# Split weights made by GpSimd for the expert blocks computed ahead, and 34 of them instead of 30

## The chip, the core and the metric

The kernel runs on one core of one Trainium2 chip. A core has a matrix engine (TensorE, PE in the rows, with its weight loads shown apart as PEld), three engines for elementwise work (VectorE or DVE, ScalarE or ACT, GpSimd or POOL), a queue engine that issues transfers (SyncE or SP) and 16 DMA engines. The metric is the device time of one execution in microseconds (us).

## The reference

One decoder layer on 512 tokens of width 1024 in float32. First a mixer (a gated linear recurrence beside sparse attention), then an expert layer, then a gated embedding. What the change touches is the expert layer:

```python
q = (xt @ wq).reshape(128, 8, 2, 128)                       # 8 heads, two half queries
s = einsum('thcd,hckd->thck', q, sub_keys)                  # key scores, 128 keys a half
top_s, top_i = top_k(s, 16)
best_s, best_c = top_k(all sums of the two halves, 16)      # 16 experts of 16384 for each token and head
expert = i1 * 128 + i2
w = softmax(best_s)
act = gelu(einsum('thkd,td->thk', u[expert], xt))
out = einsum('thk,thkd->td', w * act, v[expert])
```

## The kernel before

Tokens stand in four tiles of 128. For the last three tiles (TD = 384 tokens) nothing is gathered: the kernel multiplies all 16384 rows of u and v, in 128 blocks of 128 experts. For block b it loads uT[b] (128x1024, 512 KB, tile `ur`), forms u x for the 384 tokens in PSUM (`apsum`), takes the gelu of it on ScalarE (tile `gp` or `ga`), multiplies that by the routing weights of the block (`wt`) and multiplies the product by v[b] into six accumulators (`ac`). The first token tile is done by gathering: GpSimd issues 256 indirect loads of rows, and VectorE does a dot product or a scaled add with each.

A float32 product can be made in two ways here. With `full`, TensorE takes the float32 tiles as they are, one matmul instruction for each of the 8 chunks, which the trace shows as two records each. Otherwise a tile is split into a high part (a copy that rounds to fp32r) and a low part (what is left), and `mm3` makes three fast matmuls for each chunk: high by high, high by low, low by high. `split` (lines 186 and 187) makes the high part on ScalarE and the low part on VectorE. The tokens are split beforehand (`xTh`, `xTl`).

The stages around the change are these. After the key scores of the last head (a loop over `hc`, with the top 16 taken by VectorE on each), XB = 6 full blocks are issued behind the last score matmul. Meanwhile `route(1)` works on VectorE and ScalarE: it combines the two top-16 lists of token tile 1 and finds expert numbers. `dense_tile` for token tiles 1, 2 and 3 then turns the expert numbers into a dense weight array: VectorE makes one-hot arrays `o1`, `o2` and their products `oh`, `ol` (128x2048 f16, two buffers each), TensorE multiplies them (`wm`, lines 979 and 980), ScalarE evicts (`hn`, `stage`), a DMA writes them to DRAM (`wd`). Between two groups of 32 such matmuls a generator, `a_steps`, issues three chunks of an expert block, so that TensorE has work while it waits for one-hots; `route(2)` and `route(3)` are woven in too. For tiles 1 and 2 (FT = 3) these blocks are full, for tile 3 split. Blocks still missing up to NPRE = 30 come after, split; the last HOLD = 3 of them load and store through GpSimd's queue, all others through SP's. The gelu of the first AHEAD = 10 blocks stays in SBUF, that of blocks 10 to NPRE - 1 goes to DRAM (`gd`) and comes back. Last, a loop over all 128 blocks does the products with v and, from block NPRE on, also the split u products one block ahead; the gathering for token tile 0 is spread over blocks NPRE to 124.

`ur`, `uh` and `ul` have two buffers each, so a block's tiles wait until TensorE is done with the block two before it. Each engine runs its instructions in the order in which the scheduler wrote them. In the block below, line 783 is the full product and line 779 the split.

Of the kernel before, what the change touches and what calls it, by code (L numbers as in the profile page):

```python
# [10 lines left out]
F32 = mybir.dt.float32  # L11
# [5 lines left out]
AF = mybir.ActivationFunctionType  # L17
ALU = mybir.AluOpType
# [23 lines left out]
FT = 3  # L42
# [24 lines left out]
PLAN = [("b",0),("b",1),("c",),("a",3,(1,2,0),4),("p",),("a",3,(1,2,0),8),("a",3,(1,2,0),ALL),("l",0),("o",0,2),("o",0,0),("o",0,1),("a",2,(1,2,0),5),("a",2,(1,2,0),ALL),("o",0,3),("l",1),("a",1,(0,1,2),ALL),("o",1,3),("o",1,2),("a",0,(0,1,2),3),("a",0,(0,1,2),ALL),("o",1,1)]  # L67
POST = [("n",3),("o",0),("n",2),("n",1),("n",0)]
APRI = 150
XB = 6  # L70
NP = 3
NPRE = 30
STARTS = [sum(16 // (k + 1) for k in range(i)) for i in range(17)]
NCAND = STARTS[16]

# [79 lines left out]
def _body(ctx, tc, a, out, dbg=None):  # L155
    nc = tc.nc
    V, S, G, PE = nc.vector, nc.scalar, nc.gpsimd, nc.tensor
    act = S.activation
# [21 lines left out]
    def mm3(o, lh, ll, rh, rl, first, last):  # L180
        PE.matmul(o, lhsT=lh, rhs=rh, start=first, stop=False)  # L181
        PE.matmul(o, lhsT=lh, rhs=rl, start=False, stop=False)  # L182
        return PE.matmul(o, lhsT=ll, rhs=rh, start=False, stop=last)  # L183

    def split(hi, lo, src):
        act(hi, src, AF.Copy)  # L186
        return V.tensor_tensor(lo, src, hi.bitcast(F32), op=ALU.subtract)  # L187

    def flat(ap):
        return ap.rearrange("p a b -> p (a b)")  # L190
# [336 lines left out]
    with ExitStack() as e2:  # L527
# [170 lines left out]
        for step in PLAN:  # L698
            if step[0] == "a":
                tt, order, n = step[1:]  # L700
# [30 lines left out]
    SH = [128, QH, 16, 16]  # L731
    gd = dram.tile([max(NPRE - AHEAD, 1), 128, TD], F32, name="gd")
    wd = [dram.tile([n_, 128, TD // 32, 128], F32, name=f"wd{k}") for k, n_ in enumerate((WFIRST, NB // 4 - WFIRST))]
# [34 lines left out]
    def a_steps(full):  # L768
        b = nextb[0]
        nextb[0] += 1  # L770
        dq = nc.gpsimd if NPRE - HOLD <= b < NPRE else nc.sync
        ur = dense.tile([128, NC, 128], F32, name="ur")
        dq.dma_start(out=ur, in_=a["uT"][b])
        g_ = prep.tile([128, TD], F32, name="gp") if b < AHEAD else dense.tile([128, TD], F32, name="ga", bufs=3)
        ahead.append(g_ if b < AHEAD or b >= NPRE else None)
        if not full:
            uh = dense.tile([128, NC, 128], F32R, name="uh")
            ul = dense.tile([128, NC, 128], F32R, name="ul")
            split(flat(uh), flat(ul), flat(ur))
        o = aps.tile([128, 512], F32, name="apsum")  # L780
        for c in range(NC):
            if full:
                PE.matmul(o[:, :TD], lhsT=ur[:, c], rhs=xf[:, c], start=c == 0, stop=c == NC - 1)  # L783
            else:
                mm3(o[:, :TD], uh[:, c], ul[:, c], xTh[:, c, T - TD:], xTl[:, c, T - TD:], c == 0, c == NC - 1)
            if c < NC - 1:
                yield
        act(g_, o[:, :TD], AF.Gelu_apprx_tanh)  # L788
        if AHEAD <= b < NPRE:
            dq.dma_start(out=gd[b - AHEAD], in_=g_)  # L790

    def a_block(full=False):
        if nextb[0] < NB:
            for _ in a_steps(full):
                pass
# [71 lines left out]
    with ExitStack() as e2:  # L867
# [4 lines left out]
        with ExitStack() as e3:  # L872
# [40 lines left out]
                        V.max_index(ti[tt][:, h, 8:16], tv[tt][:, h, 8:16], rep)  # L913
            with tc.issue_after(last.ins):
                for _ in range(XB):
                    a_block(True)

        psw = e2.enter_context(tc.tile_pool(name="psw", bufs=3, space=PSUM, reuse_waits="tile"))
        rs = e2.enter_context(tc.tile_pool(name="rs", bufs=1, reuse_waits="tile"))
# [30 lines left out]
        def dense_tile(tt, nxt):  # L950
            it, wh, wl, wl32 = routed[tt]
            gen = iter(())
            for k in range(8):
# [21 lines left out]
                for g in range(2):  # L975
                    o = psw.tile([128, 8, 128], F32, name="wm")
                    for t in range(8):
                        q = 4 * g + t // 2
                        PE.matmul(o[:, t], lhsT=o2[:, q, :, t % 2], rhs=oh[:, q, :, t % 2], start=True, stop=False)
                        last = PE.matmul(o[:, t], lhsT=o2[:, q, :, t % 2], rhs=ol[:, q, :, t % 2], start=False, stop=True)  # L980
                    c0 = (k % 2) * 16 + g * 8
                    act(stage[0][:, :, c0:c0 + 8], o.rearrange("p t i -> p i t"), AF.Copy, scale=1.0 / 4096)
                    with tc.issue_after(last.ins):
                        for _ in range(NP):
                            if next(gen, 0) == 0 and nextb[0] < NPRE - HOLD:
                                gen = a_steps(tt < FT)
                                next(gen)
                if k % 2:
                    sv = stage[0].rearrange("p (b i) t -> p b (i t)", i=4)
# [15 lines left out]
        for tt in range(1, NT):  # L1005
            dense_tile(tt, route(tt + 1, rs) if tt + 1 < NT else iter(()))
        while nextb[0] < NPRE:
            a_block(FH)
# [200 lines left out]
@with_exitstack  # L1209
def tile_hybrid_block(ctx: ExitStack, tc: tile.TileContext, a, out):  # L1210
    _body(ctx, tc, a, out)
# [16 lines left out]
```

## Time and profile before

| | |
|---|---|
| median of 3 runs | 1738.25 us (1738.06 to 1745.13) |
| the profiled execution | 1738.71 us |
| its span in the trace | 1737.0 us |
| TensorE busy | 1682.5 us, 97% |
| VectorE busy | 1253.3 us, 72% |
| ScalarE busy | 742.4 us, 43% |
| GpSimd busy | 475.8 us, 27% |
| matmul records of full blocks (line 783) | 320, two for each matmul |
| high parts of split blocks on ScalarE (`uh`) | 108 |

The shares are means over stages of different kinds; the rows further down show the stages apart. A busy TensorE is not TensorE at its peak, since one matmul's end overlaps the next one's start: pace is read from start to start. In the table by stage each number of us is the time in which the engine had an instruction, and the difference to the length of the stage is idle time.

### The profile page before, as it was taken

The numbers are of one execution on the slowest core, as the hardware profiler recorded it, in microseconds if no ns is written. First come the engines' busy times: TensorE is split into PE (matmuls) and PEld (weight loads), VectorE is DVE, ScalarE is ACT, GpSimd is POOL, SyncE is SP. The second block draws the span as 40 slices with busy tenths as digits, with TensorE's granted clock in tenths as the row PEclk, the third lists the DMA queues.
The fourth block names the chain that finished last, engine by engine and source line by source line (L and its number), as shares of the span: only waits on it lengthen the run. The fifth ranks groups of instructions, "written<-read, shape, count | busy, mean of one in ns | idle before, by whom it ended". The sixth has DMA issues, their size and how long they took to land.

```text
span 1737.0 us, 24222 instructions
## 1 busy us (share of the span) xinstructions
PE 1682.5 (97%) x8959; PEld 1430.6 (82%) x8959; DVE 1253.3 (72%) x2442; ACT 742.4 (43%) x1276; POOL 475.8 (27%) x353
## 2 busy tenths in 40 slices
PE   7999999998999999999999999999999999999998
PEld 6866788877885667877899999999999999999987
DVE  5553555556999998594568877787787788888863
ACT  6432555444213985453343333333333333333342
POOL 0001300012000000100035556455554455455510
PEclk9998999889999999999999999999999999999999
DMA  7311022012212679977669888989898999999841
GB/s 254 102 49 27 28 84 63 13 51 96 73 49 62 185 233 267 317 255 253 211 232 331 319 318 324 341 307 324 326 317 315 332 322 325 348 333 336 315 133 49
DMA packets 147303, 374.30 MB, mean 215 GB/s; under 512 B 11670, under 2 KB 60438, under 8 KB 147182
## 3 DMA queue, kind: packets, MB, share of 16 engines
q1 hardware_dynamic: 108608, 232.90, 39.8%
q0 software_dynamic: 38576, 139.86, 22.7%
q8 instruction: 70, 1.15, 0.3%
q14 instruction: 49, 0.40, 0.1%
HBM read 339.42 MB, written 33.29 MB: 215 GB/s over the span
## 4 chain that ended last, share of the span: by engine, by line
PE 80%; DVE 8%; DMA 6%; ACT 3%; issue 2%; SPq 1%; POOL 0%; DVEq 0%; ACTq 0%; POOLq 0%
PE ac L183 9%; PE ac L182 9%; PE ac L181 9%; PE apsum L181 8%; PE apsum L183 8%; PE apsum L182 8%; PE mm L181 5%; PE mm L182 5%; PE mm L183 5%; PE ob L660 2%; DMA ga<-gd 2%; PE apsum L783 2%; DMA ur<-uT 2%; PE pt L657 1%; PE tp L183 1%
## 5 line engine op out<-in xcount | busy, mean ns | idle before, releaser
L183 PE MATMUL ac<-vh,pl 128*128 128x512 f32 x768 | 300.8, 392 | 2.8 <-DVE pl L187 2.8
L181 PE MATMUL ac<-vh,ph 128*128 128x512 f32 x768 | 298.1, 390 | 2.6 <-ACT ph L186 2.6
L182 PE MATMUL ac<-vl,ph 128*128 128x512 f32 x768 | 300.6, 392 | 0.0
L1032 POOL DMA_INDIRECT row<-u,eid x128 | 214.1, 1673 | 310.9 <-DVE hn L1036 243.2
L181 PE MATMUL apsum<-aTh,uh 128*128 128x384 f32 x864 | 290.8, 337 | 2.2 <-ACT ga L788 2.2
L183 PE MATMUL apsum<-aTh,ul 128*128 128x384 f32 x864 | 289.3, 335 | 1.5 <-DVE ul L187 1.4
L182 PE MATMUL apsum<-aTl,uh 128*128 128x384 f32 x864 | 288.7, 334 | 0.0
L1032 POOL DMA_INDIRECT row<-v,eid x128 | 203.7, 1592 | 186.1 <-DVE hn L1044 161.0
L186 ACT ACTIVATE uh<-ur 128x1024 fp32r<-128x1024 f32 x108 | 114.7, 1062 | 281.6 <-PE apsum L182 262.7
L187 DVE TENSOR_TENSOR ul<-ur,uh 128x1024 fp32r<-128x1024 f32 x108 | 132.1, 1224 | 87.6 <-ACT uh L186 87.3
L183 PEld LDWEIGHTS ac<-vh,pl 128*128 128x128 f32 x768 | 144.0, 188 | 34.5 <-DVE pl L187 4.2
L186 ACT ACTIVATE vh<-vr 128x1024 fp32r<-128x1024 f32 x128 | 135.4, 1058 | 86.5 <-PE ac L183 81.6
L181 PEld LDWEIGHTS ac<-vh,ph 128*128 128x128 f32 x768 | 144.1, 188 | 30.9 <-ACT ph L186 3.2
L1044 DVE SCALAR_TENSOR_TENSOR hn<-row,cw__6982,hn 128x1024 f32<-128x1024 f32 x128 | 158.3, 1280 | 14.9 <-DMA row<-v,eid 14.9
L182 PEld LDWEIGHTS ac<-vl,ph 128*128 128x128 f32 x768 | 144.0, 188 | 28.7 <-DVE vl L187 0.5
L181 PEld LDWEIGHTS apsum<-aTh,uh 128*128 128x128 f32 x864 | 162.2, 188 | 6.3 <-ACT ga L788 2.5
L182 PEld LDWEIGHTS apsum<-aTl,uh 128*128 128x128 f32 x864 | 162.3, 188 | 4.0
L183 PEld LDWEIGHTS apsum<-aTh,ul 128*128 128x128 f32 x864 | 162.2, 188 | 2.4 <-DVE ul L187 2.3
L187 DVE TENSOR_TENSOR vl<-vr,vh 128x1024 fp32r<-128x1024 f32 x128 | 156.1, 1219 | 9.9 <-ACT vh L186 9.8
L1036 DVE SCALAR_TENSOR_TENSOR hn<-row,hn 128x1024 f32<-128x1024 f32 x128 | 156.2, 1221 | 5.6 <-DMA row<-u,eid 4.2
L186 ACT ACTIVATE ph<-ga 128x384 fp32r<-128x384 f32 x118 | 62.0, 525 | 202.3 <-DVE ga L1096 147.7
L783 PE MATMUL apsum<-xf,ur 128*128 128x384 f32 x320 | 112.8, 497 | 7.7 <-DMA ur<-uT 7.7
(384 smaller groups left out, 2934.9 us busy)
## 6 DMA issues: line engine op xcount, KB each, us to landing
vr<-v SPq DMA_DIRECT2D x128, 512.0 KB, 5.5
ur<-uT SPq DMA_DIRECT2D x125, 512.0 KB, 6.6
wt<-wd SPq DMA_DIRECT2D x32, 768.0 KB, 7.4
wraw<-wi SPq DMA_DIRECT2D x24, 512.0 KB, 4.6
wd<-hn SPq DMA_DIRECT2D x5, 1664.0 KB, 8.9
wd<-stage SPq DMA_DIRECT2D x5, 1664.0 KB, 9.1
wr<-wq SPq DMA_DIRECT2D x16, 512.0 KB, 3.6
wor<-wo SPq DMA_DIRECT2D x8, 512.0 KB, 3.6
```

What stands on the lines that cost most here:

```text
L181: PE.matmul(o, lhsT=lh, rhs=rh, start=first, stop=False)
L182: PE.matmul(o, lhsT=lh, rhs=rl, start=False, stop=False)
L183: return PE.matmul(o, lhsT=ll, rhs=rh, start=False, stop=last)
L186: act(hi, src, AF.Copy)
L187: return V.tensor_tensor(lo, src, hi.bitcast(F32), op=ALU.subtract)
L657: PE.transpose(pt_ps[:, k * 128:(k + 1) * 128], P[:, k * 128:(k + 1) * 128], ident)
L660: PE.matmul(o_ps[:, h], lhsT=pt[:, k * 128:(k + 1) * 128], rhs=kv[:, k, 256 + i * 64:256 + (i + 1) * 64], start=(k == 0), stop=(k == tt))
L783: PE.matmul(o[:, :TD], lhsT=ur[:, c], rhs=xf[:, c], start=c == 0, stop=c == NC - 1)
L1032: G.indirect_dma_start(out=gt, out_offset=None, in_=table, in_offset=bass.IndirectOffsetOnAxis(ap=eid[:, slot:slot + 1], axis=0))
L1036: V.scalar_tensor_tensor(junk, gt, 1.0, xn0, op0=ALU.mult, op1=ALU.mult, accum_out=dots[:, s_:s_ + 1])
L1044: V.scalar_tensor_tensor(ak, gt, cw_[:, s_:s_ + 1], ak, op0=ALU.mult, op1=ALU.add)
```

## The change

`full` now has a third value, None. Such a block is computed with three fast matmuls a chunk, like a split block, but its low part is made by GpSimd, and its high part by ScalarE for the first XB blocks and by GpSimd for the others. All blocks that were full become blocks of this kind: those behind the key scores, which are 8 now and were 6, and the 14 woven into token tiles 1 and 2. NPRE goes from 30 to 34, so four more blocks are computed ahead, with their gelu stored in `gd`, and four fewer in the last loop. The sum `xf` of the token halves, which only full blocks read, is still made.

```diff
--- before.py
+++ after.py
@@ -67,9 +67,9 @@
 PLAN = [("b",0),("b",1),("c",),("a",3,(1,2,0),4),("p",),("a",3,(1,2,0),8),("a",3,(1,2,0),ALL),("l",0),("o",0,2),("o",0,0),("o",0,1),("a",2,(1,2,0),5),("a",2,(1,2,0),ALL),("o",0,3),("l",1),("a",1,(0,1,2),ALL),("o",1,3),("o",1,2),("a",0,(0,1,2),3),("a",0,(0,1,2),ALL),("o",1,1)]
 POST = [("n",3),("o",0),("n",2),("n",1),("n",0)]
 APRI = 150
-XB = 6
+XB = 8
 NP = 3
-NPRE = 30
+NPRE = 34
 STARTS = [sum(16 // (k + 1) for k in range(i)) for i in range(17)]
 NCAND = STARTS[16]
 
@@ -776,7 +776,14 @@
         if not full:
             uh = dense.tile([128, NC, 128], F32R, name="uh")
             ul = dense.tile([128, NC, 128], F32R, name="ul")
-            split(flat(uh), flat(ul), flat(ur))
+            if full is None:
+                if b < XB:
+                    act(flat(uh), flat(ur), AF.Copy)
+                else:
+                    G.tensor_copy(flat(uh), flat(ur))
+                G.tensor_tensor(flat(ul), flat(ur), flat(uh).bitcast(F32), op=ALU.subtract)
+            else:
+                split(flat(uh), flat(ul), flat(ur))
         o = aps.tile([128, 512], F32, name="apsum")
         for c in range(NC):
             if full:
@@ -913,7 +920,7 @@
                         V.max_index(ti[tt][:, h, 8:16], tv[tt][:, h, 8:16], rep)
             with tc.issue_after(last.ins):
                 for _ in range(XB):
-                    a_block(True)
+                    a_block(None)
 
         psw = e2.enter_context(tc.tile_pool(name="psw", bufs=3, space=PSUM, reuse_waits="tile"))
         rs = e2.enter_context(tc.tile_pool(name="rs", bufs=1, reuse_waits="tile"))
@@ -983,7 +990,7 @@
                     with tc.issue_after(last.ins):
                         for _ in range(NP):
                             if next(gen, 0) == 0 and nextb[0] < NPRE - HOLD:
-                                gen = a_steps(tt < FT)
+                                gen = a_steps(None if tt < FT else False)
                                 next(gen)
                 if k % 2:
                     sv = stage[0].rearrange("p (b i) t -> p b (i t)", i=4)
```

GpSimd's instructions between the token sums `xf` and the first gathers (`row<-u`): before, there are only a few transfers there, of the last blocks' weights (`ur`), of late parts of the dense weights (`wd1`) and of stored gelus (`gd`).

```order
L879 TENSOR_TENSOR xf_3353<-aTh_1626,aTl_1627 128x384 x8
L773 DMA ur_6851<-uT 128x1024
L991 DMA wd1_3349<-hn_6560 128x26x128
L773 DMA ur_6885<-uT 128x1024
L773 DMA ur_6919<-uT 128x1024
L991 DMA wd1_3349<-stage_6712 128x26x128
```

The same place now, at the seam between the eighth block and the next ones:

```order
L784 TENSOR_TENSOR ul_4937<-ur_4933,uh_4936 128x1024
L784 TENSOR_TENSOR ul_4970<-ur_4966,uh_4969 128x1024
L783 CAST uh_5163<-ur_5160 128x1024
L784 TENSOR_TENSOR ul_5164<-ur_5160,uh_5163 128x1024
L783 CAST uh_5252<-ur_5249 128x1024
L784 TENSOR_TENSOR ul_5253<-ur_5249,uh_5252 128x1024
```

Eight subtractions and then fourteen pairs of a copy and a subtraction now stand between `xf` and the transfers, on an engine that had nothing there.

ScalarE's instructions behind the last high part of a query (`qh`), where `route(1)` begins; `gp` is a block's gelu, `tf`, `tr`, `bf` and `ew` are steps of the routing. Before:

```order
L186 ACTIVATE qh_4657<-mm_4632 128x512
L788 ACT_TABLE_LOAD
L788 ACTIVATE gp_4737<-apsum_4738 128x384
L811 ACTIVATE tf_4823<-ti1_3551 128x256
L836 ACTIVATE tr_4888<-df_4883 128x2048
L788 ACTIVATE gp_4750<-apsum_4751 128x384
L834 ACTIVATE bf_4886<-bi_4834 128x128
```

Now:

```order
L186 ACTIVATE qh_4657<-mm_4632 128x512
L781 ACTIVATE uh_4804<-ur_4801 128x1024
L795 ACT_TABLE_LOAD
L795 ACTIVATE gp_4737<-apsum_4742 128x384
L818 ACTIVATE tf_5009<-ti1_3551 128x256
L781 ACTIVATE uh_4837<-ur_4834 128x1024
L843 ACTIVATE tr_5074<-df_5069 128x2048
L795 ACTIVATE gp_4770<-apsum_4775 128x384
L781 ACTIVATE uh_4870<-ur_4867 128x1024
L841 ACTIVATE bf_5072<-bi_5020 128x128
```

A high part of a block now stands ahead of each of several routing steps; each of them waits until TensorE has finished the block two before.

## Rows read from the trace of the kernel before

**Rows 1.** Busy time by stage; columns are named in the first line.
```profile
core 0: us, PE busy (x) PEld busy (x) DVE busy (x) ACT busy (x) POOL busy (x), PEclk, DMA share, GB/s
526.90:557.00 30.10, 26.74 (x82) 15.53 (x82) 29.93 (x185) 9.57 (x12) 0.00 (x0) 0.94 0.23 71
557.00:676.30 119.30, 111.42 (x762) 74.77 (x762) 110.60 (x252) 98.72 (x224) 0.00 (x0) 1.00 0.73 216
676.30:719.80 43.50, 43.40 (x414) 40.51 (x412) 32.91 (x29) 25.04 (x30) 2.78 (x3) 1.00 0.94 279
719.80:742.80 23.00, 18.37 (x103) 17.09 (x101) 10.52 (x11) 8.25 (x13) 3.70 (x5) 1.00 0.99 343
742.80:860.00 117.20, 112.88 (x492) 91.77 (x493) 78.07 (x182) 47.28 (x62) 5.02 (x4) 1.00 0.72 238
860.00:1650.00 790.00, 790.00 (x3997) 718.01 (x3996) 627.53 (x767) 293.60 (x389) 409.80 (x251) 1.00 0.89 319
```

**Rows 2.** TensorE in order of time: full blocks, the wait, eleven split matmuls.
```profile
526.91 23.44 PE L783 MATMUL apsum<-xf,ur 128*128 128x384 f32 x72
553.71 0.48 PE L933 MATMUL wm<-cst,f32i 128*128 128x128 f32 x1 [3.36 <-DVE f32i L930]
...
696.97 0.34 PE L182 MATMUL apsum<-aTl,uh 128*128 128x384 f32 x1
...
698.70 0.34 PE L183 MATMUL apsum<-aTh,ul 128*128 128x384 f32 x1
```

**Rows 3.** VectorE by line in 557 to 676 us, operations with two SBUF inputs.
```profile
L960 DVE TENSOR_TENSOR o<-i,it 128x2048 f16<-128x2048 f16 x20 | 24.4, 1218 | 4.7 <-ACT ol L963 4.6
L965 DVE TENSOR_TENSOR o<-i,it 128x2048 f16<-128x2048 f16 x18 | 21.9, 1217 | 0.0
L966 DVE TENSOR_TENSOR oh<-o,whh 128x2048 f16<-128x2048 f16 x18 | 21.9, 1216 | 0.3 <-PE wm L979 0.3
L964 DVE TENSOR_TENSOR ol<-o,wll 128x1024 f16<-128x1024 f16 (+2 forms) x18 | 11.2, 626 | 1.5 <-PE wm L980 1.5
L802 DVE TENSOR_TENSOR tr<-tr 128x1024 f16<-128x1024 f16 (+2 forms) x18 | 8.2, 463 | 0.1
L798 DVE TENSOR_TENSOR tr<-ge,tr 128x2048 f16<-128x2048 f16 x4 | 4.9, 1218 | 0.0
...
L846 DVE TENSOR_TENSOR ge<-bf,st 128x2048 f16<-128x2048 f16 x2 | 2.4, 1218 | 0.0
L855 DVE TENSOR_TENSOR ge<-j,io 128x2048 f16<-128x2048 f16 x2 | 2.4, 1216 | 0.0
L798 DVE TENSOR_TENSOR tr<-ge,st 128x2048 f16<-128x2048 f16 x2 | 2.4, 1214 | 0.0
```

**Rows 4.** GpSimd by line, whole span: what can price its new work.
```profile
L879 POOL TENSOR_TENSOR xf<-aTh,aTl 128x384 f32<-128x384 f32 x8 | 7.8, 1015 | 2.6 <-DVE aTl L522 2.6
...
L627 POOL TENSOR_TENSOR pc<-pc,cst 128x256 f32<-128x256 f32 x4 | 2.9, 732 | 98.3 <-ACT pc L626 98.3
...
L363 POOL MEMSET AT<- 128x256 f32 x2 | 0.6, 312 | 0.3 <-POOLq L1221 0.3
...
L1221 POOL MEMSET const-float32-0.0<- 128x1 f32 x1 | 0.1, 99 | 0.3 <-issue 0.3
```

**Rows 5.** GpSimd in order of time, two met by VectorE and two not.
```profile
119.86 1.36 POOL L176 TENSOR_TENSOR rs<-rs,mhalf 128x4 f32<-128x4 f32 x1
...
132.41 0.19 POOL L175 TENSOR_SCALAR rs<-rs 128x4 f32<-128x4 f32 x1 [10.87 <-DVE rs L419]
132.69 1.03 POOL L176 TENSOR_TENSOR rs<-rs,mhalf 128x4 f32<-128x4 f32 x1
...
148.60 0.32 POOL L175 TENSOR_SCALAR kss<-kss 128x4 f32<-128x4 f32 x1 [6.00 <-DVE kss L333]
```

**Rows 6.** VectorE in order of time at the same two moments.
```profile
119.66 0.69 DVE L386 SCALAR_TENSOR_TENSOR lf<-lf,qs 128x512 f32<-128x512 f32 x1
...
148.43 0.44 DVE L187 TENSOR_TENSOR wlo<-wraw,whi 128x280 fp32r<-128x280 f32 x1
```

## The prediction

> **What bounds the kernel now.** I read the table of busy time by stage first, then TensorE in order of time at the first blocks computed ahead, then VectorE by line in the one-hot stage, then GpSimd's prices, and last a few moments at which GpSimd and VectorE meet. The reader is to see three things in the table. From 860 to 1650 us, most of the last loop, TensorE is busy 790 of 790 us: that loop is bound by TensorE, and a matmul taken out of it is time gained [rows 1]. From 557 to 676 us, token tiles 1 and 2, VectorE is busy 110.6 of 119.3 us and TensorE 111.4: both are nearly full, and each waits a little for the other [rows 1]. From 676 to 720 us TensorE is busy 43.4 of 43.5 us, and then a tail of 103 matmuls takes 23 us with the DMA engines 99% busy [rows 1]. GpSimd has nothing between 527 and 676 us [rows 1]. That emptiness is what the change uses, so the question is whether GpSimd can work there without cost to VectorE.
>
> **What the change takes off TensorE.** A full block is 16 records; 72 of them take 23.44 us [rows 2], so 0.326 us each and 5.21 us a block. A split block is 24 matmuls; from the first to the last of the eleven shown (ten steps) lie 1.73 us [rows 2], so 0.173 us each and 4.15 us a block. Blocks that were full are 1.06 us cheaper, 21 us over 20 of them, if TensorE sets the pace where they stand. Four blocks leave the last loop, which TensorE bounds: 4 x 4.15 = 16.6 us gained there. Their cost ahead is two more blocks behind the key scores and two more in the tail.
>
> In the last loop the gathering is now spread over 91 blocks, not 95. VectorE is busy 627.5 of 790 us there [rows 1]; if all of that were gathering it would grow by 4%, to some 655 of the shortened loop. I cost it at nothing, since TensorE hides it; without that cover it would be up to 25 us. The four extra stored gelus add 0.8 MB each way on DMA, in stages at 0.66 to 0.99 of the engines; only the tail is near their limit.
>
> **The key scores' blocks.** The first 134 split matmuls, all that stand ahead of the routing's first transpose, take 134 x 0.173 = 23.2 us, as the 72 full records did. So TensorE reaches that transpose at the same moment and waits for VectorE as before: 3.36 us until 553.71 [rows 2]. The two extra blocks fill no hole that was there. The high parts that ScalarE now makes ahead of routing steps wait for TensorE to finish the block two before (535, 539, 544 us, by 4.15 us a block from 526.9), and ScalarE is busy only 9.57 of 30.1 us [rows 1]; I cost them at nothing, and up to 2 us if one of them ends later than its routing step would have begun.
>
> **GpSimd's price.** A subtraction of 128x384 takes 1015 ns and one of 128x256 732 ns [rows 4]. The slope is 2.21 ns a column, so one of 128x1024 takes 1015 + 640 x 2.21 = 2.43 us. No row shows a copy on GpSimd. Below, it is bounded by the fill of 128x256, 312 ns against 99 ns for one column [rows 4]: 0.84 ns a column, 0.95 us. Above, it is bounded by the subtraction, 2.43 us. A copy has one input and one output, between the two, and nearer to the fill in work per column; I take 1.0 us and keep both ends. The Trainium skill (GPSIMD Engine Reference, section 4.1, Engine selection) calls one-input operations roughly line-rate; at its 1.2 GHz that would be an estimate of 0.85 us, and the sum below would be about 2 us lower. No run here shows it so far. So a block of token tiles 1 and 2 costs GpSimd 3.4 us. TensorE spends at least 4.15 us on the block between, so GpSimd's speed alone does not hold TensorE up.
>
> **What it costs VectorE.** Rows show that the two engines exclude each other on something. A power of 128x4 on GpSimd takes 1.03 us when VectorE is quiet; at 119.86 us it takes 1.36 us, and a VectorE operation with two SBUF inputs of 512 columns runs from 119.66 to 120.35 us [rows 5, 6]. A small GpSimd operation of 0.19 us takes 0.32 us at 148.60 us, when such a VectorE operation runs from 148.43 us for 0.44 us [rows 5, 6]. Both extra times, 0.33 and 0.13 us, are about what was left of VectorE's reading. So GpSimd stood still while VectorE read two inputs, and at full length. The other direction, VectorE standing still behind a long GpSimd operation, is in no row, since GpSimd has had no long operation beside such VectorE work.
>
> In 557 to 676 us nearly all of VectorE's work is of that kind: the nine lines sum to 24.4 + 21.9 + 21.9 + 11.2 + 8.2 + 4.9 + 3 x 2.4 = 99.7 us of a stretch of 119.3 [rows 3], 84%. GpSimd wants 14 x 3.43 = 48 us of the same thing. Whichever of the two waits, both sums do not fit: 99.7 + 48 = 148 us, before any idle time. If VectorE waits, it is late; if GpSimd waits, its low parts are late, TensorE stops at them, and the `wm` matmuls behind them on TensorE's queue stop too, for which VectorE's one-hot buffers wait. So the term hardly depends on who wins. Of GpSimd's 48 us, 16% falls beside other VectorE work or idle time and is hidden; 40 us are not. VectorE's 8.7 us of idle time were waits for ScalarE and TensorE [rows 1, 3], which a late VectorE no longer has; between losing none and all of them the stage grows by 40 to 31 us, and I take 34. The ends of this term are -8.7 us (VectorE not touched, only its idle time gone) and +57 us (40 us, and a copy at 2.43 us adds 14 x 1.43 x 0.84 = 17 us, the hidden share taken off).
>
> The Trainium skill says the same with a rule that is sterner than my rows (SBUF — State Buffer, section Who interferes with whom): a VectorE instruction with two SBUF inputs and a GpSimd instruction that reads SBUF take one shared read interface, whoever issues first has it for the whole instruction, and the other is fully blocked. By the rows alone only GpSimd waits for VectorE, and the first rival below would still be open; by the rule the term is the one taken. The rows agree in the direction that they show; no run here shows the other.
>
> Ahead of 557 us two subtractions (fifth and sixth block, from 545 and 549 us) meet the routing's large two-input operations: 2 x 2.43 = 4.9 us, between 0 and 7. The subtractions before them meet VectorE's top-16 search, which reads one input; 0.
>
> **The sum**, against the profiled execution's 1738.7 us (its span is 1737.0; the median of the runs, 1738.25, is within half a microsecond): key-score stage +4.9; token tiles 1 and 2 +34; tile 3 0, since its blocks were split before and its GpSimd work is over; tail +5.5, as the order has 135 matmuls there against 103, 32 x 0.173, with the DMA engines full, so that no idle time of the 4.6 us there goes away; last loop -16.6. That is +27.8: **1766 us**. Its own range is 1757 to 1776.
>
> **The rivals.** First, the other side: VectorE is not held up, because GpSimd's reads give way or leave room for it. For it speaks that every VectorE duration in the rows is undisturbed. Against it speaks that GpSimd was stopped for as long as VectorE read. Its place is the stage of tiles 1 and 2, where TensorE then has 14 x 1.06 = 14.8 us less to do and VectorE's 110.6 us become the floor: -4 us, between 0 and -8.7. With +2 at the key scores, +5.5 and -16.6 it gives -13: **1725 us** (1721 to 1730). It decides as soon as GpSimd's work costs VectorE less than (16.6 - 5.5) / 14 = 0.8 us a block, of the 3.4 us that GpSimd works.
>
> Second, the thing is shared in turns within an operation, and about half of GpSimd's time is hidden: key scores +2.5, tiles 1 and 2 +17, so +8: **1747 us** (1740 to 1757). Against it: the GpSimd operations in the rows were stopped, not slowed.
>
> Third, the copy on GpSimd costs as much as the subtraction: 17 us more than the forecast, **1783 us** (1776 to 1795).
>
> **How the numbers follow.** Forecast 0.44, the first rival 0.32, the second 0.12, the third 0.12. 0.5% of the time is 8.7 us, about what a measurement of this kernel can tell from no change: 1730 to 1747. Slower by more than that are the forecast, the third rival and most of the second: 0.64. Within it lie the rest of the second and the edge of the first: 0.07. Faster is the first without that edge: 0.29. Cases of both signs hold most of the chance, so the range has to reach from the first rival to most of the third: 1721 to 1787.
>
> **What would show it.** In the trace after: the fourteen GpSimd subtractions with TensorE's and VectorE's stage of tiles 1 and 2 around 155 us long instead of 119; VectorE's 128x2048 operations on lines 967, 972 and 973 above their 1.22 us in the mean or with idle time put down to GpSimd; GpSimd's subtractions spread from 2.4 us up to some 3.6. The last loop shorter by 16 to 17 us with TensorE full. If the VectorE operations stay at 1.22 us and that stage ends earlier than before, the step on the shared reading is wrong and the first rival holds. If the stage grows while VectorE's operations keep their length and TensorE waits for `ul`, the size may be right and the loser is GpSimd. A GpSimd copy far from 1.0 us, or a last loop in which TensorE waits, would make the sum wrong elsewhere.

## The result, and the profile after

The changed kernel takes **1765.15 us** in the median (1762.35 to 1766.95), against 1738.72 for the kernel before measured beside it: a ratio of **1.0138 (95% interval 1.0120 to 1.0157)**, 1.4% slower. Its profiled execution took 1765.37 us with a span of 1763.5, against 1738.7 and 1737.0. The forecast was 1766. Its total is right, but two of its terms are off by some 9 us each, in opposite directions.

Cut at the same five places of TensorE's order of time (first block matmul; third transpose of tile 1, line 942 of the new file; last `wm`; first `ac`; last `ac`), the two spans compare as follows, in us:

```
stretch                             before   after   moved   forecast
ahead of the blocks                  526.9   524.9    -2.0       0
key scores (to the transposes)        29.8    33.0    +3.2    +4.9
tiles 1 to 3                         162.5   187.5   +25.0   +34
tail                                  23.6    31.1    +7.5    +5.5
last loop                            938.2   931.1    -7.1   -16.6
end                                   56.0    56.0     0.0       0
span                                1737.0  1763.5   +26.5   +27.8
```

The 2.0 us ahead of the blocks are scatter: that stretch ran from 519.6 to 527.3 us in the runs below, and of the change only the split of the first two blocks stands there, near 417 us. Within tiles 1 to 3 the last early block of tile 2 ends at 676.7 before and 703.1 after, so all of the +25 is in tiles 1 and 2, and tile 3 keeps its length (42.5 us before, 42.3 after). The table of busy time by stage of the changed kernel, with the columns of [rows 1], for key scores, tiles 1 and 2, tail and last loop:

```profile
524.90:557.90 33.00, 27.69 (x143) 27.00 (x143) 32.93 (x169) 16.32 (x19) 12.65 (x5) 0.90 0.22 66
...
557.90:703.10 145.20, 110.39 (x910) 102.89 (x910) 144.36 (x264) 101.23 (x226) 67.00 (x29) 0.89 0.58 175
...
745.60:776.40 30.80, 25.97 (x135) 24.69 (x135) 16.34 (x39) 10.60 (x16) 4.27 (x6) 0.94 0.97 322
776.40:1707.50 931.10, 923.76 (x4562) 823.98 (x4561) 715.89 (x941) 339.10 (x452) 428.85 (x257) 1.00 0.85 302
```

In tiles 1 and 2 VectorE is busy 144.36 of 145.2 us, where it was 110.60 of 119.3 [rows 1]: it has become the bound, by doing the same work more slowly. TensorE was spared 14.8 us of work there and is busy 110.4 us, hardly less than the 111.4 of [rows 1]: its granted clock was 0.89 in this stage, in which it stops for VectorE, and 1.00 before. VectorE by line there, which answers to [rows 3] (967, 972, 973 are the old 960, 965, 966):

```profile
L972 DVE TENSOR_TENSOR o<-i,it 128x2048 f16<-128x2048 f16 x17 | 26.8, 1574 | 0.0
L973 DVE TENSOR_TENSOR oh<-o,whh 128x2048 f16<-128x2048 f16 x17 | 25.5, 1504 | 0.0
L967 DVE TENSOR_TENSOR o<-i,it 128x2048 f16<-128x2048 f16 x18 | 23.5, 1307 | 0.0
...
L952 DVE CAST wll<-wl 128x128 f16<-128x128 f32 x3 | 3.7, 1225 | 0.0
L835 DVE FIND_INDEX8 bi<-bv,crep 128x8 uint32<-128x50 f32 x16 | 3.2, 201 | 0.0
```

The three large operations took 1.22 us each in [rows 3]; their means are now 1.31 to 1.57. The searches with one small input keep their 0.20 us. Lines of single tiles, whole span (duration in ns, shortest / median / longest):

```profile
L972 DVE TENSOR_TENSOR o<-i,it x24: 1210/1215/3422, 562.5 to 736.3; 128x2048 f16<-128x2048 f16 x24
...
L784 POOL TENSOR_TENSOR ul<-ur,uh x22: 2387/2660/3442, 416.7 to 691.9; 128x1024 fp32r<-128x1024 f32 x22
...
L783 POOL CAST uh<-ur x14: 1037/1345/4993, 563.2 to 690.6; 128x1024 fp32r<-128x1024 f32 x14
```

The median operation of VectorE is as fast as ever; a few take 2.2 us longer, which is nearly one whole GpSimd subtraction (2.39 undisturbed). GpSimd's copy takes 1.04 us undisturbed and 4.99 at worst. One moment of both engines in order of time:

```profile
596.16 4.99 POOL L783 CAST uh<-ur 128x1024 fp32r<-128x1024 f32 x1 [2.60 <-PE apsum L182]
596.17 1.20 DVE L973 TENSOR_TENSOR oh<-o,whh 128x2048 f16<-128x2048 f16 x1
...
597.30 0.68 DVE L971 TENSOR_TENSOR ol<-o,wll 128x1024 f16<-128x1024 f16 x1
...
597.90 1.22 DVE L972 TENSOR_TENSOR o<-i,it 128x2048 f16<-128x2048 f16 x1
...
599.03 1.22 DVE L853 TENSOR_TENSOR ge<-bf,st 128x2048 f16<-128x2048 f16 x1
...
600.17 0.28 DVE L848 TENSOR_REDUCE z<-ew 128x8 f32<-128x128 f32 x1
...
600.37 1.86 DVE L805 TENSOR_TENSOR tr<-ge,st 128x2048 f16<-128x2048 f16 x1
...
601.23 3.25 POOL L784 TENSOR_TENSOR ul<-ur,uh 128x1024 fp32r<-128x1024 f32 x1
...
602.26 2.76 DVE L809 TENSOR_TENSOR tr<-tr 128x1024 f16<-128x1024 f16 x1
```

While VectorE runs four two-input operations back to back from 596.17 to 600.25, GpSimd's copy stands still; it ends 0.9 us after them, when a VectorE operation with one input (600.17) has come. VectorE's next two-input operation, from 600.37, is held by the copy and takes 1.86 us in place of 1.22. The subtraction waits for that one in turn (3.25 us in place of 2.39, until 604.48), and VectorE's 128x1024 operation behind it, 0.68 us by itself, takes 2.76. TensorE pays at the start of the next tile, not at the blocks. Its two largest waits in tiles 1 to 3 (us in total, times, longest) are for VectorE's tile indices and products; no wait of its matmuls for `ul` is listed there, and its weight loads waited for `ul` once, 0.2 us:

```profile
PE wm L940 <- DVE f32i L937: 20.3, 2, 11.2
...
PE wm L987 <- DVE ol L971: 6.2, 2, 5.6
```

### The profile page after: what moved, and what is told of

Read it like the earlier page. It is cut to its first block, busy times and chain, and to the rows that moved or that the text cites. A ratio compares the mean times of both kernels' runs of the same rounds, so it can differ in the third digit from the quotient of the medians.

```text
span 1763.5 us, 24650 instructions
## 1 busy us (share of the span) xinstructions
PE 1677.6 (95%) x9119; PEld 1463.5 (83%) x9119; DVE 1292.8 (73%) x2440; ACT 746.0 (42%) x1282; POOL 570.6 (32%) x389
## 4 chain that ended last, share of the span: by engine, by line
PE 53%; DMA 14%; DVE 13%; issue 12%; POOL 4%; ACT 2%; SPq 0%; POOLq 0%; DVEq 0%; ACTq 0%
DMA row<-v,eid 8%; PE ac L183 5%; PE ac L182 5%; PE ac L181 5%; PE apsum L181 4%; PE apsum L183 4%; PE apsum L182 4%; PE mm L181 4%; PE mm L182 4%; PE mm L183 4%; POOL row L1039 4%; PE ob L660 2%; DMA ga<-gd 2%; DMA row<-u,eid 1%; DVE o L972 1%
## 5 line engine op out<-in xcount | busy, mean ns | idle before, releaser
L181 PE MATMUL apsum<-aTh,uh 128*128 128x384 f32 x1024 | 351.6, 343 | 6.5 <-ACT gp L795 3.8
L183 PE MATMUL apsum<-aTh,ul 128*128 128x384 f32 x1024 | 347.1, 339 | 2.1 <-DVE ul L187 2.1
L182 PE MATMUL apsum<-aTl,uh 128*128 128x384 f32 x1024 | 346.2, 338 | 0.0
L1039 POOL DMA_INDIRECT row<-u,eid x128 | 218.1, 1704 | 304.2 <-DVE hn L1043 245.2
L1039 POOL DMA_INDIRECT row<-v,eid x128 | 210.2, 1642 | 175.3 <-DVE hn L1051 151.2
L181 PEld LDWEIGHTS apsum<-aTh,uh 128*128 128x128 f32 x1024 | 195.3, 191 | 10.9 <-ACT gp L795 4.1
L182 PEld LDWEIGHTS apsum<-aTl,uh 128*128 128x128 f32 x1024 | 195.5, 191 | 3.8
L183 PEld LDWEIGHTS apsum<-aTh,ul 128*128 128x128 f32 x1024 | 195.2, 191 | 3.3 <-DVE ul L187 3.1
L1051 DVE SCALAR_TENSOR_TENSOR hn<-row,cw__7518,hn 128x1024 f32<-128x1024 f32 x128 | 158.9, 1282 | 35.6 <-DMA row<-v,eid 35.5
L187 DVE TENSOR_TENSOR pl<-ga,ph 128x384 fp32r<-128x384 f32 x118 | 65.8, 558 | 58.8 <-ACT ph L186 58.8
```

What stands on the lines that cost most here:

```text
L1039: G.indirect_dma_start(out=gt, out_offset=None, in_=table, in_offset=bass.IndirectOffsetOnAxis(ap=eid[:, slot:slot + 1], axis=0))
L1051: V.scalar_tensor_tensor(ak, gt, cw_[:, s_:s_ + 1], ak, op0=ALU.mult, op1=ALU.add)
```

## The experiments

All of them in the stretches of the table above, from one profiled execution each (us; "waits" are TensorE's listed waits in the last loop). A profiled execution can stand some us off its kernel's median: with fills 1747.5 for 1737.0, with idle fills 1732.8 for 1738.7. The medians and ratios in the text are against runs of the kernel before on the same chip.

```
kernel                     key scores  tiles 1-3   tail   last loop  waits
before                        29.8       162.5     23.6     938.2     4.3
after                         33.0       187.5     31.1     931.1     7.1
fills, no reading             33.0       158.0     31.0     941.5    14.6
before + idle reading         29.9       189.0     24.0     937.9     3.9
before + idle fills           29.8       162.6     24.4     938.4     3.4
before + idle copies          29.8       186.4     23.5     940.6     4.9
after, counts of before       33.9       182.6     23.0     939.0     3.6
before, counts of after       29.9       175.0     31.1     932.2     7.7
after, tiles full again       33.0       168.3     37.7     926.5     4.6
after, high part ScalarE      33.0       198.1     31.9     931.3     7.4
after, gathering spread       33.0       187.6     31.2     945.8    17.4
after, fewer gathers          33.0       187.7     30.7     928.3     6.8
after, plain transfers        33.1       187.0     31.5     920.6     1.5
before, four blocks split     28.6       162.8     23.8     941.0     5.9
```

**Is it the reading?** The theory is that of the prediction; its rival is that GpSimd's time as such, or the handover, holds the stage up. Three runs take them apart: the changed kernel with GpSimd busy as long, but not reading; and the kernel before with GpSimd reading, or filling, for nobody.

```diff
                     act(flat(uh), flat(ur), AF.Copy)
+                    G.tensor_tensor(flat(ul), flat(ur), flat(uh).bitcast(F32), op=ALU.subtract)
                 else:
-                    G.tensor_copy(flat(uh), flat(ur))
-                G.tensor_tensor(flat(ul), flat(ur), flat(uh).bitcast(F32), op=ALU.subtract)
+                    G.memset(flat(uh).bitcast(F32), 0.03)
+                    G.tensor_copy(flat(uh)[:, 0:1], flat(ur)[:, 0:1])
+                    for _ in range(3):
+                        G.memset(flat(ul).bitcast(F32), 0.0001)
```

> The changed kernel, but in the 14 blocks ahead of token tiles 1 and 2 GpSimd fills the high part (one 128x1024 fill and a one-column copy) and the low part (three fills) in place of copying and subtracting: as many microseconds of GpSimd (four fills of 128x1024, about 3.7 us a block by 0.84 ns a column), the same buffers and handovers, but next to nothing read from SBUF. The right weights of these blocks are left out. Theory (GpSimd's reading and VectorE's two-input reading exclude each other): the stage of tiles 1 and 2, 145.2 us in the changed kernel, falls to between 112 and 121 us, VectorE's lines 967, 972 and 973 go back to a mean of 1.22 us, and the total falls to between 1730 and 1742 us. Rival (GpSimd's time, its place in the chain or its queue holds the stage up): 1765 within 5 us, VectorE's operations at 1.22 us with idle time ahead of them. Third possibility (writing counts like reading): VectorE's operations stay at 1.5 us.

Measured: 1736.98 us, 0.9981 (0.9967 to 0.9995) of before. GpSimd worked 67.4 us between 558 and 703 us (67.0 in the changed kernel), all 56 fills among it, and tiles 1 to 3 took 158.0 us, 29.5 less than in the changed kernel. VectorE by line there (970, 975 and 976 are 967, 972 and 973):

```profile
L975 DVE TENSOR_TENSOR o<-i,it 128x2048 f16<-128x2048 f16 x24 | 29.2, 1217 | 0.0
L976 DVE TENSOR_TENSOR oh<-o,whh 128x2048 f16<-128x2048 f16 x24 | 29.2, 1217 | 2.2 <-PE wm L989 2.2
L970 DVE TENSOR_TENSOR o<-i,it 128x2048 f16<-128x2048 f16 x24 | 29.2, 1216 | 0.0
```

The fills of `ul`, three in four of all (ns, shortest / median / longest, and their first and last start):

```profile
L787 POOL MEMSET ul<- x42: 947/954/1033, 563.6 to 663.7; 128x1024 f32 x42
```

All back at 1.22 us. Time on GpSimd, writing and the handover cost VectorE nothing; what is left is the reading. The other two put the same work beside the full blocks of the kernel before (`full == "r"` in tiles 1 and 2):

```diff
+        if full == "r":
+            uh = dense.tile([128, NC, 128], F32R, name="uh")
+            ul = dense.tile([128, NC, 128], F32R, name="ul")
+            G.tensor_copy(flat(uh), flat(ur))
+            G.tensor_tensor(flat(ul), flat(ur), flat(uh).bitcast(F32), op=ALU.subtract)
```

> The kernel before, all its blocks as they were, and beside each full block of token tiles 1 and 2 GpSimd copies and subtracts the same 128x1024 weights into buffers that nothing uses. Theory (shared reading): VectorE is late although nobody needs GpSimd's result; the stage of tiles 1 and 2 grows from 119.9 to between 140 and 155 us, and the total from 1738.7 to between 1758 and 1773 us. Rival (the loss is in TensorE waiting for low parts, or in the order of split blocks): no change, 1738.7 within 4 us.

Measured: 1764.76 us, 1.0146 (1.0112 to 1.0180). The stretch grew by 26.5 us with no one waiting for GpSimd, and VectorE's lines show it:

```profile
L970 DVE TENSOR_TENSOR o<-i,it 128x2048 f16<-128x2048 f16 x23 | 36.2, 1572 | 0.0
L971 DVE TENSOR_TENSOR oh<-o,whh 128x2048 f16<-128x2048 f16 x24 | 34.3, 1430 | 2.9 <-PE wm L984 2.9
```

> As the kernel before with idle GpSimd work beside it, but with four fills of 128x1024 and a one-column copy in place of the copy and the subtraction: GpSimd busy as long, reading next to nothing. Theory (shared reading): 1738.7 within 4 us. Rival (any GpSimd work there, its writes or its buffers, costs): as much as the run with the copy and subtraction, some 20 to 30 us.

Measured: 1738.66 us, 0.9986 (0.9969 to 1.0004), and 162.6 us for tiles 1 to 3. This run shows less than it was meant to: its fills of `ul` wait for no block, and they ran a hundred microseconds ahead of the stage:

```profile
L786 POOL MEMSET ul<- x42: 957/994/1013, 411.4 to 449.1; 128x1024 f32 x42
```

Of 56 fills only 12 stood beside the routing, with 14 copies of one column. That fills cost VectorE nothing therefore rests on the changed kernel with fills, where all 56 started between 562 and 664 us. With that run and the one with idle reading the loss of the stage is shown to be VectorE held up by GpSimd's reading.

**Does a copy count like a subtraction?** The same idle work, with two more copies in place of the subtraction:

```diff
-            G.tensor_tensor(flat(ul), flat(ur), flat(uh).bitcast(F32), op=ALU.subtract)
+            for _ in range(2):
+                G.tensor_copy(flat(ul), flat(ur))
```

> The kernel before with idle GpSimd work beside the 14 full blocks of tiles 1 and 2, but three copies with one SBUF input each (3 x 1.04 us a block undisturbed) in place of the copy and the subtraction, to buffers that nothing uses. If any reading by GpSimd excludes VectorE's two-input operations, the term goes by GpSimd's reading time, whatever the operation: 14 x 3.1 x 0.84 = 37 us at most, and by the price that the run with copy and subtraction showed (26 of 48 us) some 20 to 28; total 1756 to 1767 us, VectorE's lines with two inputs above 1.22 us in the mean. If a copy with one input leaves VectorE alone: 1738 within 4 us, VectorE at 1.22.

Measured: 1761.62 us, 1.0126 (1.0105 to 1.0146); tiles 1 to 3 longer by 23.9 us. The copies read for 42 x 1.04 = 43.7 us, copy and subtraction for 48.0, and the stage grew by 55% of it in both runs (23.9 and 26.5 us): GpSimd's reading time decides, not the operation. The two engines in order of time show how it goes:

```profile
561.45 6.10 POOL L783 CAST uh<-ur 128x1024 fp32r<-128x1024 f32 x1 [144.08 <-DMA ur<-uT]
...
568.07 2.06 DVE L971 TENSOR_TENSOR o<-i,it 128x2048 f16<-128x2048 f16 x1
570.05 2.05 DVE L972 TENSOR_TENSOR oh<-o,whh 128x2048 f16<-128x2048 f16 x1
570.97 2.03 POOL L783 CAST uh<-ur 128x1024 fp32r<-128x1024 f32 x1
...
572.21 1.86 DVE L966 TENSOR_TENSOR o<-i,it 128x2048 f16<-128x2048 f16 x1
572.95 2.02 POOL L785 CAST ul<-ur 128x1024 fp32r<-128x1024 f32 x1
```

From 568 us they take whole operations in turn: 1.22 us of VectorE, 1.04 of GpSimd, each standing still for the other, so that both take 2.0. VectorE never took more than 2.06 us on these lines in this run, one operation of its own and one copy; with subtractions it was 3.4.

**GpSimd's share halved.** If GpSimd's reading is the price, moving the copies to ScalarE should take some of it away.

```diff
-                if b < XB:
-                    act(flat(uh), flat(ur), AF.Copy)
-                else:
-                    G.tensor_copy(flat(uh), flat(ur))
+                act(flat(uh), flat(ur), AF.Copy)
```

> The changed kernel with the high parts of the 14 blocks of tiles 1 and 2 made by ScalarE too, so that GpSimd only subtracts there: its reading falls from 48 to 34 us. Theory (the sum of VectorE's two-input work and GpSimd's reading is the floor): the stage of tiles 1 and 2 shortens by 14 x 1.0 x 0.84 = 12 us, from 145 to 133, and the total falls to 1751 to 1758 us. Rival (a one-input copy on GpSimd costs VectorE nothing, the subtraction alone does): 1765 within 4 us. Rival (ScalarE, 101 us busy in that stage, becomes late): 1765 or more, with TensorE or VectorE waiting for ScalarE.

Measured: 1776.44 us, 1.0207 (1.0175 to 1.0239): 11 us slower still, which the third possibility had. TensorE now waits for both parts of the weights, and GpSimd for ScalarE:

```profile
POOL ul L781 <- ACT uh L780: 97.6, 15, 12.6
...
PE apsum L183 <- POOL ul L781: 22.6, 10, 5.2
...
PE apsum L181 <- ACT uh L780: 8.2, 5, 3.4
```

In the changed kernel copy and subtraction followed each other on GpSimd; here each subtraction starts only when ScalarE's queue, between `wm` evictions, reaches the copy. So this run does not price the copy: it made a new chain.

**The counts.** Once with GpSimd's split weights and the old counts, once with full products and the new ones:

```diff
-XB = 8
+XB = 6
-NPRE = 34
+NPRE = 30
```

> The changed kernel with the counts of before: split weights by GpSimd, but six blocks behind the key scores and 30 in all. It prices the counts: by the prediction's terms they are worth -16.6 (last loop) + 5.5 (tail) + 4.9 (key scores), so this kernel would be 6 us slower than the changed one, 1771. By the stretches that the two traces show (loop -5.2, tail +7.4, key scores +1.2) it would be 3 us faster, 1762. The stage of tiles 1 and 2 stays at 140 to 148 us by either; if the counts were behind its growth it would be back at 120 and the total near 1738.

Measured: 1764.53 us, 1.0141 (1.0109 to 1.0174), within a microsecond of the changed kernel. Beside GpSimd's split the new counts are worth nothing; the prediction had them at a gain of 6 us.

> The kernel before with the new counts alone: eight blocks behind the key scores and 34 in all, those of the key scores and of tiles 1 and 2 still full, no work for GpSimd. Stage of tiles 1 and 2 as before (119.9 us) by every theory. Two full blocks more behind the key scores: 10.4 us, of which 3.4 fill the wait for VectorE, so +7; tail +5.5 to +7.4. By the prediction's term the last loop loses 16.6: 1738.7 + 7 + 6 - 17 = 1735 us. By the rival (with 34 blocks ahead the gathering, squeezed on fewer blocks, makes TensorE wait, as in the changed kernel and in the run with fills): last loop -7 to +3, and 1744 to 1754 us, with TensorE idle in the loop 7 us or more, not 4.

Measured: 1751.03 us, 1.0079 (1.0047 to 1.0110). The last loop lost 6.0 us of its 938.2, not 16.6, and TensorE's waits in it rose from 4.3 to 7.7; the rival holds. My +7 for the two full blocks was low and in the wrong stretch: the key scores kept their 29.8 us, and tiles 1 to 3 grew by 12.5.

```diff
-                                gen = a_steps(None if tt < FT else False)
+                                gen = a_steps(tt < FT)
```

> The changed kernel, but with full products again in the 14 blocks of tiles 1 and 2: split weights by GpSimd only behind the key scores, with the new counts. Stage of tiles 1 and 2 back at 120 us by the theory of shared reading. With the stretches of the changed kernel for the rest (key scores +1.2, tail +7.4, last loop -5) 1738.7 + 4 = 1742 us; with the prediction's terms (+4.9, +5.5, -16.6) 1732.5 us.

Measured: 1749.08 us, 1.0057 (1.0040 to 1.0074). Above both figures: tiles 1 to 3 took 168.3, and not 162.5, where TensorE had 53 split records more and 20 full ones fewer (2.7 us by their spacing) and the eighth block's subtraction held one VectorE cast for 2.2 us, and the tail took 37.7 us at a granted clock of 0.82. GpSimd's split of the eight blocks behind the key scores is worth 2 us against the run before it, less than these measurements tell apart; splitting tiles 1 and 2 as well costs 16 (14 by the ratios).

**The last loop.** The theory: the gathering, on 91 blocks in place of 95, comes late in it. The chain in the changed kernel at one wait, VectorE first, then ScalarE and TensorE:

```profile
1565.95 1.28 DVE L1051 SCALAR_TENSOR_TENSOR hn<-row,cw__7518,hn 128x1024 f32<-128x1024 f32 x1 [2.61 <-DMA row<-v,eid]
...
1569.42 1.22 DVE L187 TENSOR_TENSOR ul<-ur,uh 128x1024 fp32r<-128x1024 f32 x1
1570.56 0.55 DVE L1103 TENSOR_TENSOR ga<-ga,wt 128x384 f32<-128x384 f32 x1
...
1571.14 0.52 ACT L186 ACTIVATE ph<-ga 128x384 fp32r<-128x384 f32 x1 [5.41 <-DVE ga L1103]
...
1571.72 0.50 PE L181 MATMUL ac<-vh,ph 128*128 128x512 f32 x1 [1.80 <-ACT ph L186]
...
1573.33 0.63 PE L182 MATMUL ac<-vl,ph 128*128 128x512 f32 x1
```

VectorE stands 2.61 us for a gathered row, is behind with `ga` by that, and TensorE stops for 1.80. After it the `ac` matmuls take 0.63 us and start 0.43 apart, where they start 0.23 apart otherwise. The busy time of that stretch, columns as above, has the granted clock at 0.68, so part of it at the lower level of 1.2 GHz:

```profile
1571.70:1577.00 5.30, 5.28 (x16) 4.05 (x17) 5.30 (x6) 2.23 (x3) 2.97 (x2) 0.68 1.00 386
```

Waits and such slow matmuls, taken as all that the steps from one matmul's start to the next have above their usual 0.23 or 0.17 us, add up to 12.6 us in this loop and 5.8 before. Where they stand tells more: before, all 5.8 lie ahead of 832 us, at the loop's begin; now 5.8 lie there too, up to 910 us, and the other 6.8 from 1519 to 1645 us, where rows of `v` are gathered. The three TensorE waits listed there, at 1553, 1572 and 1641 us, each come 4 to 6 us after a wait of VectorE for such a row, of 2.6 to 2.9 us.

```diff
-CPRE = 0.0
+CPRE = 0.5
```

> The changed kernel with the gathering spread over the blocks of the last loop that were computed ahead as well, at half the rate per block (16% fewer gathers in each later block). Theory (the last loop's gain is lost because GpSimd's gathers, packed on 91 blocks, come late there): TensorE's idle time in the loop falls from 7 to 4 us or less, and the total by 3 to 8 us, to 1757 to 1762. Rival (it is the stored gelus and v blocks that come late at the loop's begin, on full DMA engines): no gain or a loss, 1765 to 1775, with more idle time before 900 us.

Measured: 1780.45 us, 1.0240 (1.0209 to 1.0271), worse than either expectation. Of its 17.4 us of waits 11.0 come up to 920 us, where the stored gelus are fetched too (3.3 in the changed kernel), so the loop's begin has no room. The other 6.4 come from 1505 us on (3.8 in the changed kernel): fewer gathers for each later block brought nothing there, which speaks against the theory as it was put.

```diff
-                    rows[k] = gather(fetch[k][1], a[fetch[k][0]])
+                    rows[k] = rows[k - 1] if k % 16 == 15 else gather(fetch[k][1], a[fetch[k][0]])
```

> The changed kernel without 16 of the 256 gathers of the last loop (one in sixteen; VectorE uses the row fetched before instead, so that its work is the same; the right rows of these slots are left out). Gathers per block fall from 2.8 to 2.64, under the 2.69 of the kernel before. Theory (the second floor of the last loop is the fetching of the gathered rows): TensorE's idle time in the loop falls from 7 to 4 us or less, the loop from 931 to 924 to 927 us, as 80 matmuls x 0.174 = 14 us under the 938 of before, and the total to 1757 to 1762. Rival (the loop's idle time comes from the stored gelus, the v blocks or the one-hot sums): loop 930 to 935 us, total 1765 within 4.

Measured: 1764.25 us, 1.0149 (1.0121 to 1.0177). The loop fell to 928.3 us, between the two expectations, with 6.8 us of waits, and the total didn't move. VectorE's waits for rows of `v` fell from 35.5 to 23.2 us, and what the loop lost behind 1500 us from 6.8 to 3.5. That fits rows that come late. But the kernel before, with more gathers per block, lost nothing there, which speaks against a plain limit on gathers per block: inconclusive.

```diff
-            G.indirect_dma_start(out=gt, out_offset=None, in_=table, in_offset=bass.IndirectOffsetOnAxis(ap=eid[:, slot:slot + 1], axis=0))
+            G.dma_start(out=gt, in_=table[slot * 128:(slot + 1) * 128, :])
```

> The changed kernel with 256 plain transfers of the same size in place of the gathers, issued by GpSimd at the same places (contiguous rows in place of the chosen ones, so the right rows are left out): as many bytes, less of GpSimd's time per transfer (1.7 us for a gather). If GpSimd's own time per gather is what makes the rows late: loop 924 to 927 us, as without one gather in sixteen. If it is the bytes on the DMA engines (busy 90% there): loop 930 us or more, total 1765 within 4.

Measured: 1754.55 us, 1.0086 (1.0058 to 1.0113), 10.6 us less than the changed kernel (9 by the ratios); the loop 920.6 us with 1.5 us of waits. VectorE's waits for rows of `v` in the loop, first the changed kernel, then the one with plain transfers, each with GpSimd's issue (ns, shortest / median / longest):

```profile
DVE hn L1051 <- DMA row<-v,eid: 35.5, 18, 3.2
...
L1039 POOL DMA_INDIRECT row<-v,eid x128: 932/1679/3635, 1301.9 to 1684.6; - x128
```

```profile
DVE hn L1051 <- DMA row<-v: 1.3, 2, 1.0
...
L1039 POOL DMA_DIRECT2D row<-v x128: 531/531/540, 1297.6 to 1669.6; - x128
```

Nearly as many bytes and packets in the loop (132 MB for 135 on GpSimd's queue), and the waits are gone: it is the gather as GpSimd issues it, and not the bytes on the DMA engines. Whether GpSimd's 1.7 us, the chosen rows' places in memory, or the later start of each gather does it, this run does not part, since it changes all three: a plain transfer needs no expert number, and the first four rows were fetched from 629 us on.

**A better version?** By the theory, subtractions that end before the routing's two-input operations are free. The kernel before with the branch for `full is None`, used for four of its six blocks:

```diff
-                for _ in range(XB):
-                    a_block(True)
+                for i in range(XB):
+                    a_block(None if i < 4 else True)
```

> The kernel before (six blocks behind the key scores, 30 in all, full products) with GpSimd's split weights for the first four blocks alone, whose subtractions end before the routing's two-input VectorE operations begin. By the theory of shared reading: key scores 29.8 us as before (not 33.0, as in every run with six subtractions there), and 4 x 1.06 = 4.2 us of TensorE's time less, part of it taken by VectorE's own floor: 1734 to 1739 us against 1738.3. Rival (any subtraction behind the key scores delays the routing): key scores 32 to 33 us, total 1738 to 1741.

Measured: 1738.68 us, 0.9987 (0.9971 to 1.0003). The key scores took 28.6 us, so these four cost nothing, but the 1.2 us gained do not show in the total. No run that keeps all the products beat the kernel before by an amount that can be told from none.

## Why the prediction was right, and where it was not

**GpSimd's prices** held: copy 1.04 us (taken 1.0), subtraction 2.39 (2.43), fill 0.96 (0.95). The third rival falls with the first of these prices. The Trainium skill's line on one-input operations (GPSIMD Engine Reference, section 4.1, Engine selection), by which I had estimated 0.85, came out 18% under the copy that the trace shows.

**VectorE held up by GpSimd's reading** was the step on which the forecast stood, and it held: the run with idle reading and the changed kernel with fills show it from both sides. The two moments from which it was taken were thin: the 0.33 and 0.13 us that GpSimd lost were only two thirds and half of what was left of VectorE's operations (0.49 and 0.27 us), and no row had VectorE waiting. The rule of the Trainium skill (SBUF — State Buffer, section Who interferes with whom) had it for whole instructions, and both traces above agree: VectorE is held by one GpSimd operation at a time, up to 2.06 us with copies and 3.4 with subtractions. In equal shares an operation of 1.22 us could not take longer than 2.44, so the 3.4 excludes the second rival's sharing within an operation. Not all of that rule fits: the copies at 596.16 and, with idle copies, at 561.45 stood still through three and five VectorE operations that began after them. The fills agree with its other half, that only a GpSimd instruction that reads contends.

**The size of that term** was too large, 34 for a measured 25. The step that was mis-sized is "16% falls beside other VectorE work or idle time and is hidden": VectorE's busy time grew from 111.19 us (of 120.0, to 676.7 us) to 144.36 (of 145.2), by 33.2 us and not 40, so 15 of GpSimd's 48 us, 31%, cost VectorE nothing. Part of the reason is probably what the moment above shows: VectorE keeps the reading while such operations follow back to back, and GpSimd gets it when a gap or a one-input operation comes. The other half, VectorE's idle time, came out at the end that I had named and not taken: it went from 8.8 to 0.8 us. 33.2 - 8.0 = 25.2.

**Key scores**: 3.2 for 4.9. One of the two subtractions met routing work as described, and the operation that it met, 0.21 us by itself at 553.30, took 2.38, for which ScalarE's next step waited 3.07 us:

```profile
546.88 2.88 POOL L784 TENSOR_TENSOR ul<-ur,uh 128x1024 fp32r<-128x1024 f32 x1 [5.82 <-ACT uh L781]
...
547.45 2.38 DVE L811 TENSOR_TENSOR j<-tr 128x128 f16<-128x128 f16 x1
...
549.87 1.91 ACT L859 ACTIVATE tr<-tf 128x2048 f16<-128x2048 f16 x1 [3.07 <-DVE j L811]
...
553.30 0.21 DVE L811 TENSOR_TENSOR e<-tr 128x128 f16<-128x128 f16 x1
```

Every run with subtractions behind the fourth block shows 33.0 to 33.9 us here, every run without them 28.6 to 29.9.

**Tile 3** at nothing was right. **The tail** grew by 7.5, not 5.5: its 32 matmuls were counted rightly and its idle time stayed (4.6 us before, 4.8 after), but TensorE, after waits of 1.86 and 2.71 us, had a granted clock of 0.94 in it, not 1.00.

**The last loop** is the large miss, -7.1 for -16.6. First the count: 16 of the 24 matmuls of block 30 stood in the tail before, so the loop has 2256 block matmuls in place of 2336, and 80 x 0.1736 = 13.9 us was all there was to gain. Then the cover: that the gathering costs nothing, "since TensorE hides it", was not so. Waits and the slow matmuls behind them rose by 12.6 - 5.8 = 6.8 us, and -13.9 + 6.8 is the -7.1 that was measured. With plain transfers they are 2.4, and the loop's 17.6 us less is 13.9 + 3.4 and 0.3 more. In the runs with all gathers on 91 blocks, the late part of the loop lost 4.4 to 16.8 us, in the six with 95 blocks 0 to 2.6. Why four blocks make that difference stays open.

So 9 us too much loss in one term and 9.5 us too much gain in another cancelled: the mechanism was right, but that the total came out within a microsecond is luck. The **first rival** had VectorE right for the case that it describes, -4 us in tiles 1 to 3 and -4.5 in the run with fills, but with the same loop term it said 1725, and that run took 1737. Had reading been free, the forecast's own sum would have missed by 10 (by the ratio) to 12 us.

## What to carry to other kernels

Before work is moved to an idle GpSimd, ask of the engine beside it how much of its time goes to operations with two SBUF inputs. Where VectorE is near its limit with them, most of GpSimd's reading time (here 33 of 48 us) comes back as VectorE time, whoever uses the result, while fills cost it nothing. Where a loop is bound by one engine and a second stream of work has to keep up beside it (here the gathered rows), count which instructions really stand in the loop, and try what shortening it does to the second stream before booking the whole of what is taken out.

## What the runs showed that was not expected

VectorE can keep the reading over operations that follow at once: GpSimd's copy of 1.04 us took 4.99 beside four VectorE operations, and 6.10 in another run, while elsewhere the two took turns; what decides between these is not shown. Some VectorE casts with a single input were held as well: the 128x128 cast of line 952, f32 to f16, took 0.22 us before and 1.23 in the mean after. And a short wait of TensorE costs more than its length: 1.80 us at 1571.72 was followed by matmuls at nearly twice their spacing, so that in this loop 7.1 us of waits came to 12.6.
